# A hybrid transformer block with expert retrieval on one core: gate tables built beside 59 blocks in place of 83, weight splits three pieces ahead, and a rearranged end

## The chip, the cores and the metric

The kernel runs on one core of one Trainium2 chip. The metric is the device time of one launch in microseconds. Engines: TensorE (PE, with PEld for its weight loads), VectorE (DVE), ScalarE (ACT), GpSimd (POOL) and SyncE (SP). They run their own instruction streams and meet at semaphores; transfers between DRAM and the on-chip memory are queued by SP, ACT and POOL.

## The reference

For 512 tokens of width 2048: an input projection, a gated MLP over chunks and a windowed attention in parallel, an output projection with residual, and then the part that takes most of the time, a mixer that retrieves 128 of 16384 experts for each token:

```python
def peer(h, w_query, sub_keys, expert_down, expert_up):
    q = (xf @ w_query).reshape(T, PEER_HEADS, 2, D_QUERY // 2)
    s1 = jnp.einsum('thd,kd->thk', q[:, :, 0], sub_keys[0])
    s2 = jnp.einsum('thd,kd->thk', q[:, :, 1], sub_keys[1])
    v1, i1 = lax.top_k(s1, PEER_TOPK)
    v2, i2 = lax.top_k(s2, PEER_TOPK)
    cand = (v1[..., :, None] + v2[..., None, :]).reshape(T, PEER_HEADS, PEER_TOPK * PEER_TOPK)
    top_v, flat = lax.top_k(cand, PEER_TOPK)
    experts = e1 * N_KEYS + e2
    gates = jax.nn.softmax(top_v, axis=-1)
    ...
        u = jnp.take(expert_down, ec, axis=0)
        a = jax.nn.gelu(jnp.einsum('cd,chkd->chk', xc, u), approximate=False)
        vt = jnp.take(expert_up, ec, axis=0)
        return jnp.einsum('chk,chkd->cd', gc * a, vt)
```

After it the residual is added and a last norm gives the output. Everything is float32.

## The kernel before, in words

**Two ways through the experts.** 352 tokens (`TD`) go through all 16384 experts densely: 128 blocks `down(b)` of 128 experts each (`a = gelu(h @ down)`), and 16 chunks `up(c)` of 8 blocks each, which multiply `gate * a` with the `up` weights into the accumulator `accT`. The gate is zero where an expert was not chosen. The other 160 tokens (a full block of 128 and one of 32) fetch only the rows that they chose, in 640 *units*: one indirect transfer of 512 KB by POOL (L706) and one VectorE instruction over 128x1024 (L720 for the down rows, L732 for the up rows). The units are two jobs, 512 for the block of 128 tokens and then 128 for the 32. A unit's row lands in one of 4 buffers `row` or, once the tables are done, one of `MORE_ROWS` = 4 buffers `more`.

**The weight stream.** Every dense product is made of three float32r products (L166, L167, L168) from halves `hi` and `lo` of weight and data. `Stream` brings the weights in pieces of 512 KB: SP loads `wraw`, ScalarE casts it to `whi` (L143), and VectorE or GpSimd subtracts to get `wlo` (L145; a *split* below). A block takes 2 pieces and 48 matmuls of 352 columns, a chunk 16 pieces and 4 *quarters* of 96 matmuls. `W.get()` hands out a piece and has the next 2 split; each kind of buffer holds 4.

**Gate tables.** 88 *quads* of 4 tokens: 4 VectorE instructions `p2` (L860), 4 Abs and one Relu on ScalarE (L865, L867), 8 products on TensorE (L873) and 2 copies on ScalarE into `stage` (L886), which go to `g_dram`. They are run beside the first `OPEN` blocks. In a chunk, `make_ga` multiplies `a` by the gate (VectorE, L994), casts to `gah` (ScalarE, L998) and subtracts to `gal` (VectorE, L999).

**Order.** TensorE's order is written out: `NPRE` blocks first, their `a` spilled to `a_dram` and read back later, then chunks, with the remaining blocks between chunks, 8 for each, once a chunk needs them. After block `OPEN - 1` the table buffers are released, and the accumulator, the gates' buffers and `more` are allocated in their place (`open_late`).

**Pacing.** `Pace` decides what stands in the other engines' streams between TensorE's groups. `vector` is a balance of VectorE time: each group of matmuls adds 0.98 of its own time, each piece of work takes its estimate off. `use_pool` gives a split to GpSimd when the balance is at or below zero, and GpSimd's own balance allows. A unit is emitted when `gap` ns of TensorE work have gone by since the last. A table step is emitted when its share of the time left to `OPEN` has gone by.

```python
    def use_pool(self):
        if self.vector > 0.0 or self.pool < 0.0:
            self.vector -= 1250.0
            return False
```

**The end.** In the last chunk, `rows_out(q)` turns a finished quarter of `accT` back to rows on TensorE (tile `dn`, 2 buffers, L1145), VectorE adds the residual (`xr`, L1148), ScalarE squares for the norm (L1135) and `gf` is multiplied in (L1137). `last_norm` scales and sends a token block out (L1122 to L1131). `rest_of_first` does that for the 128 fetched tokens in quarter 1 (`yf`, L1160), `rest_of_last` for the 32 in quarter 3: their sums lie in four parts, which are brought by 8 transfers and added by 8 VectorE instructions (L1184).

Of the kernel before, what the change touches and what calls it, by code (L numbers as in the profile page):

```python
# [19 lines left out]
P = 128  # L20
D = 2048
# [15 lines left out]
NCHUNK = NK // CB  # L37
NPRE = 88
OPEN = NPRE - 5
TG = 32  # L40
NTG = TD // TG
BIG = 3.0e38
COL_NS = 0.4505
MORE_ROWS = 4


class Pace:


    def __init__(self):  # L50
        self.hot, self.paced, self.units = deque(), deque(), deque()
        self.later = []
        self.vector = self.pool = self.wait = self.due = self.left = 0.0
        self.gap = 2600.0
        self.held = False
# [4 lines left out]
    def use_pool(self):  # L60
        if self.vector > 0.0 or self.pool < 0.0:
            self.vector -= 1250.0
            return False
        self.vector -= 500.0
        self.pool -= 2500.0
        return True
# [8 lines left out]
    def step(self, ns):  # L75
        self.vector = max(min(self.vector + 0.98 * ns, 3000.0), -4000.0)
        self.pool = min(self.pool + ns, 3000.0)
# [80 lines left out]
def block_kernel(ctx, tc, a, out):  # L158
# [675 lines left out]
    def table(b, choice):  # L834
# [15 lines left out]
        def quad(n):  # L850
            def f():
# [17 lines left out]
                def products():  # L869
# [5 lines left out]
                    if n % 8 == 0:  # L875
                        if "pool" not in stage:
                            psc.release()
                            stage["pool"] = tc.alloc_tile_pool(name="pst", bufs=1, side="right",
                                                               reuse_waits="tile")
                        for h in range(2):  # L880
                            stage[h] = stage["pool"].tile([P, NK // 2, TG], F32, name="stage",
                                                          bufs=4)
                    o = 4 * (n % 8)
# [4 lines left out]
                    if n % 8 == 7:  # L888
                        for h in range(2):
# [98 lines left out]
    def make_ga(b):  # L988
        if b not in a_sb:
            return  # L990
        t = a_sb.pop(b)
        t3 = t.rearrange("p (g t) -> p g t", g=NTG)
        g = g4[b // 4][:, :, (b % 4) * TG:(b % 4 + 1) * TG]
        nc.vector.tensor_tensor(t3, t3, g, op=OP.mult)  # L994
        pace.spend(1060.0)
# [19 lines left out]
    def down(b):  # L1015
        ps = ps2.tile([P, TD], F32, name="dn", bufs=2)
        for h in range(2):
            hi, lo = W.get()
            for k in range(8):
# [22 lines left out]
    def up(c):  # L1042
# [3 lines left out]
        for q in range(4):  # L1046
# [14 lines left out]
            for i in range(2):  # L1061
                w = W.get()
                for j in (2 * i, 2 * i + 1):
# [7 lines left out]
                tick()  # L1071
            if last and q == 1:
                rest_of_first()
            if last and q == 2:
                pace.drain()
                rest_of_last = finish_last()
            if last and q == 3:
                rest_of_last()
            if last and q:
# [4 lines left out]
            w = [W.get(1), W.get(2)]  # L1084
            for m in range(4):
                for j in range(4, 8):
                    multiply(m, j, w[j // 2 - 2])
                y = accT[:, 4 * q + m, :]
                if c == 0:
                    nc.scalar.copy(y, ps[m])  # L1090
                else:
                    nc.vector.tensor_add(y, ps[m], y)  # L1092
                    pace.spend(520.0)
            if nxt is not None and q == 3:
                for j in range(6, 8):
# [43 lines left out]
    def rows_out(q):  # L1139
        cols = slice(q * 512, (q + 1) * 512)  # L1140
        for b in range(ND):
# [7 lines left out]
            square(b, n, y, q, nc.vector if q == 3 else nc.gpsimd)  # L1149
            if q == 3:  # L1150
                last_norm(b, n, y, o_rows[b + 1][:n])

# [12 lines left out]

    def finish_last():
        n = EX
        x = late["fin"].tile([P, D], F32, name="xf")
        nc.scalar.dma_start(x[:n], x_dram[NB - 1][P - n:])
        parts = []  # L1170
        for h in range(2):
            cols = slice(h * D // 2, (h + 1) * D // 2)
            for s in range(P // EX):
                if h:
                    t = pg.tile([P, D // 2], F32, name="row", bufs=4)
                else:
                    t = late["p"].tile([P, D // 2], F32, name="more", bufs=MORE_ROWS)
                eng = nc.sync if s % 2 else nc.scalar
                eng.dma_start(t[:n], y_dram[1][s * n:(s + 1) * n, cols])
                parts.append((t, cols))  # L1180

        def rest():
            for t, cols in parts:
                nc.vector.tensor_add(x[:n, cols], x[:n, cols], t[:n])  # L1184
            for q in range(4):
                square(NB, n, x, q, nc.vector)
            last_norm(NB, n, x, o_rows[NB - 1][P - n:])
        return rest

    def spread():  # L1190
        left = sum(2 * 24 for k, i in order if k == "d" and i >= OPEN)
        left += sum(384 for k, i in order if k == "u")
        pace.gap = (left * TD * COL_NS - 45e3) / len(pace.units)

    for kind, i in order:
        if kind == "u":
            up(i)
            continue
        down(i)
        if i == OPEN - 1:  # L1200
# [3 lines left out]
            open_late()  # L1204
            spread()
            opening.extend([
# [82 lines left out]
```

## Time and profile before

| what | value |
| --- | --- |
| median of 3 runs | 3058.1 us (3056.44 to 3060.74) |
| the profiled execution | 3053.1 us, of which the trace spans 3051.4 us |
| TensorE busy / VectorE / GpSimd / ScalarE | 2867.4 / 2260.2 / 1474.2 / 1152.7 us |
| bytes moved | 779.91 MB, mean 256 GB/s |
| mean granted TensorE clock | 0.976 |

Busy time is that of the engine's own instructions. In the rows below, a window's columns are its width, each engine's busy time with the number of instructions, the granted clock as a share of full speed, the share of the 16 DMA engines' time that was busy, and GB/s.

### The profile page before, as it was taken

The page shows a single profiled execution, that of the slowest core. Times are in us where ns is not written, and L with a number is a line of the kernel's source. Part 1 is how long each engine was busy: PE and PEld are TensorE (multiplying, and loading weights), DVE is VectorE, ACT ScalarE, POOL GpSimd, SP SyncE. Part 2 cuts the span into 40 slices and gives each one's busy share as a digit, 9 for nine tenths or more (in the row PEclk, how much of TensorE's full clock was granted, in tenths as well). Part 3 has the DMA queues.
Part 4 walks back from the last instruction along what each step waited for, and adds up shares of the span by engine and source line. Part 5 has one row for each costly group of instructions (what it writes and reads, how often), then busy time and mean ns, then how long its engine had stood idle before and what let it go on. Part 6 is the DMA issues. An engine that isn't in the chain of part 4 may idle for free. (4 is left out here: it accounts for less than half of the span.)

```text
span 3051.4 us, 44502 instructions
## 1 busy us (share of the span) xinstructions
PE 2867.4 (94%) x16925; PEld 2727.1 (89%) x16925; DVE 2260.2 (74%) x3359; ACT 1152.7 (38%) x1932; POOL 1474.2 (48%) x998
## 2 busy tenths in 40 slices
PE   7999999999999899999989999999999999999976
PEld 6888878799999899999988999998999999999975
DVE  3125642469947999999957888887788889778865
ACT  3244432222333456767824222322232323323223
POOL 2132100123578667777645666666665444344432
PEclk9999999999999999999999999999999999999987
DMA  5221242422379678978798999999989999899983
GB/s 191 86 83 56 76 162 90 146 90 87 122 260 343 215 264 293 317 261 316 264 333 323 357 347 342 337 334 329 353 330 347 334 334 360 315 332 335 347 306 104
DMA packets 265190, 779.91 MB, mean 256 GB/s; under 512 B 25488, under 2 KB 94416, under 8 KB 259408
## 3 DMA queue, kind: packets, MB, share of 16 engines
q1 hardware_dynamic: 151952, 382.75, 36.7%
q0 software_dynamic: 92160, 335.59, 29.0%
q10 hardware_dynamic: 20864, 58.74, 5.0%
q8 instruction: 133, 2.18, 0.3%
q14 instruction: 81, 0.66, 0.1%
HBM read 726.20 MB, written 50.77 MB: 255 GB/s over the span
## 5 line engine op out<-in xcount | busy, mean ns | idle before, releaser
L145 POOL TENSOR_TENSOR wlo<-wraw,whi 128x1024 fp32r<-128x1024 f32 x284 | 701.0, 2477 | 849.1 <-ACT whi L143 813.3
L143 ACT CAST whi<-wraw 128x1024 fp32r<-128x1024 f32 x628 | 641.2, 1048 | 679.3 <-PE up L167 326.8
L168 PE MATMUL up<-gah,wlo 128*128 128x352 f32 x2048 | 673.9, 329 | 47.2 <-POOL wlo L145 44.0
L166 PE MATMUL up<-gah,whi 128*128 128x352 f32 x2048 | 675.2, 330 | 19.9 <-DVE accT L1092 19.2
L145 DVE TENSOR_TENSOR wlo<-wraw,whi 128x1024 fp32r<-128x1024 f32 x344 | 462.1, 1350 | 305.5 <-ACT whi L143 303.8
L166 PE MATMUL dn<-h2d,whi 128*128 128x352 f32 x2048 | 667.3, 326 | 15.2 <-ACT whi L143 15.2
L168 PE MATMUL dn<-h2d,wlo 128*128 128x352 f32 x2048 | 669.7, 327 | 5.8 <-POOL wlo L145 3.6
L167 PE MATMUL up<-gal,whi 128*128 128x352 f32 x2048 | 668.9, 327 | 0.0
L167 PE MATMUL dn<-h2d,whi 128*128 128x352 f32 x2048 | 667.0, 326 | 0.0
L168 PEld LDWEIGHTS up<-gah,wlo 128*128 128x128 f32 x2048 | 394.0, 192 | 56.9 <-POOL wlo L145 53.2
L166 PEld LDWEIGHTS up<-gah,whi 128*128 128x128 f32 x2048 | 394.4, 193 | 27.5 <-DVE accT L1092 18.0
L166 PEld LDWEIGHTS dn<-h2d,whi 128*128 128x128 f32 x2048 | 390.8, 191 | 16.1 <-ACT whi L143 16.1
L168 PEld LDWEIGHTS dn<-h2d,wlo 128*128 128x128 f32 x2048 | 389.5, 190 | 10.3 <-POOL wlo L145 6.9
L167 PEld LDWEIGHTS up<-gal,whi 128*128 128x128 f32 x2048 | 394.7, 193 | 0.0
L167 PEld LDWEIGHTS dn<-h2d,whi 128*128 128x128 f32 x2048 | 389.7, 190 | 0.0
L720 DVE SCALAR_TENSOR_TENSOR row<-row,half_row 128x1024 f32<-128x1024 f32 x236 | 282.6, 1211 | 70.0 <-DMA row<-in_down_rows,idx 55.7
L860 DVE SCALAR_TENSOR_TENSOR p<-iota,eT,gT 128x256 fp32r<-128x256 f32 x352 | 317.0, 959 | 1.9 <-PE tr L873 1.9
L706 POOL DMA_INDIRECT row<-in_down_rows,idx x236 | 249.3, 1056 | 140.5 <-DVE row L720 88.7
L706 POOL DMA_INDIRECT more<-in_up_rows,idx x160 | 184.4, 1152 | 162.0 <-DVE half_row L732 136.3
L706 POOL DMA_INDIRECT row<-in_up_rows,idx x160 | 182.9, 1143 | 145.3 <-DVE half_row L732 115.7
L732 DVE SCALAR_TENSOR_TENSOR half_row<-more,wgt,half_row 128x1024 f32<-128x1024 f32 x160 | 205.1, 1282 | 1.5 <-DMA more<-in_up_rows,idx 0.3
L732 DVE SCALAR_TENSOR_TENSOR half_row<-row,wgt,half_row 128x1024 f32<-128x1024 f32 x156 | 200.0, 1282 | 1.7 <-DMA row<-in_up_rows,idx 0.3
(201 smaller groups left out, 3755.7 us busy)
## 6 DMA issues: line engine op xcount, KB each, us to landing
wraw<-in_down SPq DMA_DIRECT2D x256, 512.0 KB, 5.6
wraw<-in_up SPq DMA_DIRECT2D x256, 512.0 KB, 7.0
wraw<-in_win SPq DMA_DIRECT2D x52, 512.0 KB, 3.8
g_dram<-stage ACTq DMA_DIRECT2D x22, 1024.0 KB, 8.2
g<-g_dram SPq DMA_DIRECT2D x32, 704.0 KB, 9.3
wraw<-in_wout SPq DMA_DIRECT2D x32, 512.0 KB, 3.7
wraw<-in_wq SPq DMA_DIRECT2D x32, 512.0 KB, 3.7
aa<-a_dram SPq DMA_DIRECT2D x88, 176.0 KB, 9.1
```

The costliest lines, as they stand in the source:

```text
L143: self.nc.scalar.copy(hi, src)
L145: eng.tensor_sub(lo, src, hi.bitcast(F32))
L166: nc.tensor.matmul(ps, wh, xh, start=start, stop=False)
L167: nc.tensor.matmul(ps, wh, xl, start=False, stop=False)
L168: nc.tensor.matmul(ps, wl, xh, start=False, stop=stop)
L706: nc.gpsimd.indirect_dma_start(out=t, out_offset=None, in_=src, in_offset=bass.IndirectOffsetOnAxis(ap=idx[i][:, j, h:h + 1], axis=0))
L720: nc.vector.scalar_tensor_tensor(t, t, 1.0, half_row, op0=OP.mult, op1=OP.mult, accum_out=dots[i][:, j, h:h + 1])
L732: nc.vector.scalar_tensor_tensor(half_row, t, wgt[i][:, j:j + 1], half_row, op0=OP.mult, op1=OP.add)
L860: nc.vector.scalar_tensor_tensor(p2[:, j], iota[:, None, :].to_broadcast([P, 2, P]), t[:, 1, k:k + 1], hl[:, k, :, None].to_broadcast([P, ...
```

## The change

`NPRE` goes from 88 to 64, and `OPEN`, which is `NPRE - 5`, from 83 to 59. So the same 88 quads stand beside 59 blocks, 24 fewer `a` tiles are spilled and read back, chunks start 24 blocks earlier, and chunks 7 to 14 have 8 blocks between them in place of chunks 10 to 14. `W.get(3)` asks for three splits ahead instead of two in `down` and in the first half of a quarter. In `Pace` the refill goes from 0.98 to 1.12 and the threshold of `use_pool` from 0 to -300, which leaves more splits on VectorE; during the last two groups of a quarter nothing is emitted (`held`). The gap of units is 2300 in place of 2600 while the tables are made, and is worked out anew at each chunk from what is left. `MORE_ROWS` is 3. In the last chunk `rest_of_first` moves from quarter 1 to quarter 2; the four parts of the 32 tokens are brought by 2 transfers and summed by 4 products with a matrix of ones, one ahead of each group of quarter 3; and the three last norms stand behind all three last adds. `NTG` and `FULL` change nothing at 352 = 11 x 32 tokens.

```diff
-NPRE = 88
+NPRE = 64
 OPEN = NPRE - 5
...
-MORE_ROWS = 4
+MORE_ROWS = 3
...
-        self.gap = 2600.0
+        self.gap = 2300.0
...
-        if self.vector > 0.0 or self.pool < 0.0:
+        if self.vector > -300.0 or self.pool < 0.0:
...
-        self.vector = max(min(self.vector + 0.98 * ns, 3000.0), -4000.0)
+        self.vector = max(min(self.vector + 1.12 * ns, 3000.0), -4000.0)
...
-            hi, lo = W.get()
+            hi, lo = W.get(3)
...
-                w = W.get()
+                w = W.get(3)
...
-            if last and q == 1:
+            if last and q == 2:
                 rest_of_first()
-            if last and q == 2:
                 pace.drain()
-                rest_of_last = finish_last()
-            if last and q == 3:
-                rest_of_last()
+                steps_of_last.extend(finish_last())
...
             for m in range(4):
+                pace.held = m > 1
+                if last and q == 3 and steps_of_last:
+                    steps_of_last.pop(0)()
...
-            if q == 3:
-                last_norm(b, n, y, o_rows[b + 1][:n])
+        if q == 3:
+            for b in range(ND):
+                n = min(P, TD - b * P)
+                last_norm(b, n, late["x"][b], o_rows[b + 1][:n])
...
+        def piece(q):
+            cols = slice(q * 512, (q + 1) * 512)
+            ps = ps2.tile([P, 512], F32, name="dn", bufs=2)
+            nc.tensor.matmul(ps[:n], ones, parts[q // 2][:, q % 2 * 512:(q % 2 + 1) * 512],
+                             start=True, stop=True)
+            nc.vector.tensor_add(x[:n, cols], ps[:n], x[:n, cols])
+            square(NB, n, x, q, nc.gpsimd)
+            if q == 3:
+                last_norm(NB, n, x, o_rows[NB - 1][P - n:])
...
+    def spread(at):
+        left = sum(48 if k == "d" else 384 for k, i in order[at:]) * TD * COL_NS
+        if pace.units:
+            pace.gap = max(2000.0, (left - 110e3) / len(pace.units))
```

What stands in GpSimd's stream at the start of chunk 5, before (`DMA` rows are units' transfers, `wlo` is a split):

```order
L706 DMA row<-in_up_rows,idx_4077 128x1024 x2
L145 TENSOR_TENSOR wlo<-wraw,whi 128x1024
L706 DMA row<-in_up_rows,idx_4077 128x1024
L706 DMA more<-in_up_rows,idx_4077 128x1024 x2
L145 TENSOR_TENSOR wlo<-wraw,whi 128x1024
L706 DMA more<-in_up_rows,idx_4077 128x1024 x2
L706 DMA row<-in_up_rows,idx_4077 128x1024 x4
L145 TENSOR_TENSOR wlo<-wraw,whi 128x1024
```

The same chunk on GpSimd after the change (the units are earlier ones, of the down rows):

```order
L707 DMA row<-in_down_rows,idx_4077 128x1024
L146 TENSOR_TENSOR wlo<-wraw,whi 128x1024
L707 DMA row<-in_down_rows,idx_4077 128x1024 x3
L707 DMA more<-in_down_rows,idx_4077 128x1024 x3
L707 DMA row<-in_down_rows,idx_4077 128x1024 x4
L146 TENSOR_TENSOR wlo<-wraw,whi 128x1024
L707 DMA more<-in_down_rows,idx_4077 128x1024
L146 TENSOR_TENSOR wlo<-wraw,whi 128x1024
```

In the whole chunk 8 splits stood on GpSimd and 8 on VectorE; now 3 and 13, with 23 units both times. Over the kernel GpSimd's splits go from 284 to 166 and VectorE's from 344 to 462.

VectorE's stream beside the last table blocks, before: quads alternate with units, and only the last ten quads follow one another.

```order
L720 SCALAR_TENSOR_TENSOR row,dots_4083<-row,half_row 128x1024
L860 SCALAR_TENSOR_TENSOR p_13318<-iota,eT,gT 128x256 x4
L720 SCALAR_TENSOR_TENSOR row,dots_4083<-row,half_row 128x1024
L860 SCALAR_TENSOR_TENSOR p_13377<-iota,eT,gT 128x256 x4
L720 SCALAR_TENSOR_TENSOR row,dots_4083<-row,half_row 128x1024
L860 SCALAR_TENSOR_TENSOR p_13432<-iota,eT,gT 128x256 x4
L860 SCALAR_TENSOR_TENSOR p_13466<-iota,eT,gT 128x256 x4
```

The same place after the change, with what stands ahead of it:

```order
L721 SCALAR_TENSOR_TENSOR row,dots_4083<-row,half_row 128x1024
L861 SCALAR_TENSOR_TENSOR p_10829<-iota,eT,gT 128x256 x4
L861 SCALAR_TENSOR_TENSOR p_10873<-iota,eT,gT 128x256 x4
L848 TENSOR_TENSOR gT<-tr,gT 128x128
L146 TENSOR_TENSOR wlo<-wraw,whi 128x1024
L861 SCALAR_TENSOR_TENSOR p_10931<-iota,eT,gT 128x256 x4
L861 SCALAR_TENSOR_TENSOR p_10954<-iota,eT,gT 128x256 x4
```

From there 34 quads follow one another with no unit and no VectorE split between them: 4 to a block in the last 8 table blocks (51 to 58), whose 16 splits all stand on GpSimd. Of the 640 units 153 stood ahead of the end of the tables, and 85 do now; the last stood in the last chunk, and now stands in block 121.

The last rows of VectorE's stream, before (`xr` by token block, 128, 128 and 96 rows):

```order
L1092 TENSOR_TENSOR accT<-up,accT 128x352 x4
L1148 TENSOR_TENSOR xr_26854<-dn,xr_26854 128x512
L1137 TENSOR_TENSOR xr_26854<-xr_26854,gf 128x512
L1122 TENSOR_REDUCE sf<-ss_26853 128x1
L1128 TENSOR_SCALAR xr_26854<-xr_26854,rstd 128x1024
L1148 TENSOR_TENSOR xr_26856<-dn,xr_26856 128x512
L1137 TENSOR_TENSOR xr_26856<-xr_26856,gf 128x512
```

And after the change:

```order
L1156 TENSOR_TENSOR xr_26812<-dn,xr_26812 128x512
L1145 TENSOR_TENSOR xr_26812<-xr_26812,gf 128x512
L1156 TENSOR_TENSOR xr_26814<-dn,xr_26814 128x512
L1145 TENSOR_TENSOR xr_26814<-xr_26814,gf 128x512
L1156 TENSOR_TENSOR xr_26816<-dn,xr_26816 96x512
L1145 TENSOR_TENSOR xr_26816<-xr_26816,gf 96x512
L1130 TENSOR_REDUCE sf<-ss_26811 128x1
L1136 TENSOR_SCALAR xr_26812<-xr_26812,rstd 128x1024
L1130 TENSOR_REDUCE sf<-ss_26811 128x1
L1136 TENSOR_SCALAR xr_26814<-xr_26814,rstd 128x1024
```

The adds of all three blocks stand first, each still followed at once by its own `gf` product; the reduces and scales follow one block after the other.

## Rows read from the trace of the kernel before

**Rows 1.** Windows of the stages: tables, opening with chunk 0, chunks 1–9, rest, last.

```profile
784.00:1540.50 756.50, 733.61 (x4699) 728.32 (x4699) 674.65 (x991) 430.22 (x885) 558.55 (x318) 0.98 0.78 271
1540.50:1666.50 126.00, 108.62 (x626) 105.64 (x624) 83.09 (x124) 40.27 (x60) 51.88 (x43) 0.92 0.95 350
1666.50:2287.60 621.10, 577.42 (x3456) 565.47 (x3457) 511.75 (x638) 181.79 (x221) 396.19 (x275) 0.97 0.91 339
2287.60:2929.10 641.50, 622.43 (x3842) 618.20 (x3841) 542.71 (x619) 200.00 (x245) 288.41 (x242) 0.99 0.93 337
2929.10:3051.40 122.30, 73.81 (x434) 71.65 (x432) 69.61 (x83) 35.95 (x62) 27.24 (x28) 0.80 0.48 175
```

**Rows 2.** Windows: ten blocks, a block with four quads' products, a quarter.

```profile
791.72:868.52 76.80, 76.80 (x482) 76.80 (x481) 52.06 (x83) 26.24 (x32) 50.63 (x20) 1.00 0.48 161
1510.31:1521.58 11.27, 11.27 (x82) 11.27 (x82) 10.84 (x17) 10.19 (x27) 5.20 (x2) 1.00 0.81 299
1961.08:1976.36 15.28, 15.28 (x99) 15.28 (x97) 14.27 (x13) 3.24 (x4) 11.02 (x10) 1.00 1.02 397
```

**Rows 3.** TensorE's waits, whole span: us in total, times, longest us.

```profile
PE up L168 <- POOL wlo L145: 44.0, 25, 3.8
PE dn L1145 <- DVE xr L1148: 25.6, 4, 16.1
```

**Rows 4.** Timeline of VectorE and GpSimd, a table block: start, us, instruction, idle ahead.

```profile
1031.85 6.43 DVE L860 SCALAR_TENSOR_TENSOR p<-iota,eT,gT 128x256 fp32r<-128x256 f32 x4
1039.35 1.66 DVE L860 SCALAR_TENSOR_TENSOR p<-iota,eT,gT 128x256 fp32r<-128x256 f32 x4
1031.73 2.38 POOL L145 TENSOR_TENSOR wlo<-wraw,whi 128x1024 fp32r<-128x1024 f32 x1
```

**Rows 5.** Groups, chunk 5 and then 2488.5 to 2612: busy us, mean ns, idle ahead.

```profile
L145 DVE TENSOR_TENSOR wlo<-wraw,whi 128x1024 fp32r<-128x1024 f32 x8 | 16.7, 2088 | 1.0 <-ACT whi L143 1.0
L999 DVE TENSOR_TENSOR gal<-aa,gah 128x352 fp32r<-128x352 f32 x8 | 4.2, 526 | 4.7 <-ACT gah L998 4.7
...
L145 DVE TENSOR_TENSOR wlo<-wraw,whi 128x1024 fp32r<-128x1024 f32 x30 | 36.5, 1220 | 4.8 <-ACT whi L143 4.4 <-PE dn L168 0.4
```

**Rows 6.** Waits of SP's queue in chunk 5 (L132 loads a piece).

```profile
SPq L132 <- POOL wlo L145: 28.8, 8, 6.7
```

**Rows 7.** Windows: chunk 5, chunk 10, eight blocks with chunk 12.

```profile
1942.70:2011.60 68.90, 63.75 (x385) 62.60 (x385) 59.37 (x64) 19.82 (x24) 45.17 (x32) 0.98 0.92 339
2295.70:2363.80 68.10, 63.49 (x385) 62.62 (x385) 56.95 (x56) 18.06 (x19) 38.99 (x32) 0.97 0.98 362
2612.00:2751.00 139.00, 127.80 (x770) 126.40 (x770) 113.46 (x169) 43.94 (x53) 58.04 (x50) 0.96 0.92 326
```

**Rows 8.** The page's DMA queues: pieces and loads (q1), units (q0).

```profile
q1 hardware_dynamic: 151952, 382.75, 36.7%
q0 software_dynamic: 92160, 335.59, 29.0%
```

**Rows 9.** Windows: quarters 1 and 3 of the last chunk.

```profile
2949.40:2984.43 35.03, 18.96 (x109) 18.67 (x109) 18.35 (x20) 9.60 (x20) 9.44 (x9) 0.76 0.54 212
3001.57:3029.27 27.70, 18.84 (x112) 18.53 (x111) 19.04 (x24) 7.30 (x17) 4.50 (x5) 0.82 0.05 10
```

**Rows 10.** Timeline of VectorE in the last chunk and the end.

```profile
2963.82 2.29 DVE L1160 TENSOR_TENSOR yf<-yf,xf 128x2048 f32<-128x2048 f32 x1 [7.72 <-DMA xf<-x_dram]
2972.84 0.75 DVE L1128 TENSOR_SCALAR yf<-yf,rstd 128x1024 f32<-128x1024 f32 x1 [3.51 <-POOL rstd L1126]
3004.48 4.95 DVE L1184 TENSOR_TENSOR xf<-xf,more 32x1024 f32<-32x1024 f32 x4
...
3030.22 0.69 DVE L1148 TENSOR_TENSOR xr<-dn,xr 128x512 f32<-128x512 f32 x1 [0.42 <-PE dn L1145]
3031.76 0.69 DVE L1137 TENSOR_TENSOR xr<-xr,gf 128x512 f32<-128x512 f32 x1 [0.85 <-ACT junk L1135]
3033.47 0.75 DVE L1128 TENSOR_SCALAR xr<-xr,rstd 128x1024 f32<-128x1024 f32 x1 [0.95 <-POOL rstd L1126]
```

More of the change, by code (lines that the diff above doesn't have):

```diff
@@ L37 @@
 NCHUNK = NK // CB
-NPRE = 88
+NPRE = 64
 OPEN = NPRE - 5
 TG = 32
-NTG = TD // TG
+NTG = -(-TD // TG)
+FULL = TD // TG
 BIG = 3.0e38
 COL_NS = 0.4505
-MORE_ROWS = 4
+MORE_ROWS = 3
 class Pace:
@@ L882, in products @@
                                                           bufs=4)
+                            used = TD - b * P - 4 * n
+                            if used < TG:
+                                nc.gpsimd.memset(stage[h][:, :, used:], 0.0)
                     o = 4 * (n % 8)
@@ L887, in products @@
                                        ps[:, :, k].rearrange("p t k -> p k t"))
-                    if n % 8 == 7:
+                    if n % 8 == 7 or 4 * (n + 1) == TD - b * P:
                         for h in range(2):
@@ L991, in make_ga @@
         t = a_sb.pop(b)
-        t3 = t.rearrange("p (g t) -> p g t", g=NTG)
         g = g4[b // 4][:, :, (b % 4) * TG:(b % 4 + 1) * TG]
-        nc.vector.tensor_tensor(t3, t3, g, op=OP.mult)
+        if FULL < NTG:
+            end = t[:, FULL * TG:]
+            nc.gpsimd.tensor_tensor(end, end, g[:, FULL, :TD - FULL * TG], op=OP.mult)
+        t3 = t[:, :FULL * TG].rearrange("p (g t) -> p g t", g=FULL)
+        nc.vector.tensor_tensor(t3, t3, g[:, :FULL], op=OP.mult)
         pace.spend(1060.0)
@@ L1093, in up @@
                     pace.spend(520.0)
+            pace.held = False
             if nxt is not None and q == 3:
@@ L1171, in finish_last @@
         for h in range(2):
[L1172 to L1195, printed above, removed]
+            t = pg.tile([P, D // 2], F32, name="row", bufs=4)
+            nc.sync.dma_start(t, y_dram[1][:, h * D // 2:(h + 1) * D // 2])
+            parts.append(t)
+        ones = late["fin"].tile([P, EX], F32, name="ones")
+        nc.vector.tensor_reduce(ones, ident.rearrange("p (s m) -> p m s", m=EX), axis=AX.X, op=OP.add)
+        def piece(q):
[7 more added lines that the diff above has]
+                last_norm(NB, n, x, o_rows[NB - 1][P - n:])
+        return [lambda q=q: piece(q) for q in range(4)]
+    steps_of_last = []
+    def spread(at):
+        left = sum(48 if k == "d" else 384 for k, i in order[at:]) * TD * COL_NS
+        if pace.units:
+            pace.gap = max(2000.0, (left - 110e3) / len(pace.units))
+    for at, (kind, i) in enumerate(order):
         if kind == "u":
+            spread(at)
             up(i)
@@ L1204, in block_kernel @@
             open_late()
-            spread()
+            spread(at)
             opening.extend([
```

## The prediction

> **What bounds the kernel now.** I read the windows of the stages first [rows 1]: TensorE is busy for 86 to 97% of each up to 2929 us, VectorE for 89% of the table stage, and the DMA engines for 0.91 to 0.95 after it. So TensorE's work is the floor, and what can be won is the time it loses. Its work has a measured pace where nothing disturbs it: a block takes 7.68 us (ten in 76.80), a quad's products add 0.90 to a block ((11.27 - 7.68) / 4), a quarter takes 15.28, so a chunk 61.1 [rows 2]. The change leaves this work as it is, but for 4 small products. I therefore keep a ledger of lost time: a stage's width less this pace.
>
> - Tables, blocks 0 to 82 with 88 quads: 756.5 - 637.4 - 79.2 = 39.9.
> - Opening, 5 blocks and chunk 0: 126.0 - 38.4 - 61.1 = 26.5.
> - Chunks 1 to 9, nothing between them: 621.1 - 549.9 = 71.2, or 7.9 each.
> - 40 blocks and chunks 10 to 14: 641.5 - 307.2 - 305.5 = 28.8, of which 139.0 - 122.6 = 16.4 in the period of chunk 12, where the second job of units begins [rows 7].
> - Chunk 15: its window runs to 3029.3, so 100.1 - 61.1 = 39. The tail after TensorE: 22.1.
>
> That is 227.5 of the span of 3051.4 [rows 1, 2]. The waits then say on whom [rows 3]: the `up` products wait 44.0 us for splits on GpSimd, and the turned rows of the end (`dn`) 25.6 us in 4 waits for VectorE.
>
> **Why a split on GpSimd hurts.** Beside GpSimd's splits, a VectorE split takes 2088 ns on the mean; in a stretch of 123.5 us where all are on VectorE, 1220 [rows 5]. Four `p2` take 6.43 us while a split of 2.38 us starts on GpSimd, and 1.66 without one [rows 4]. So the two engines hinder each other, and eight splits of a chunk moved to GpSimd save VectorE little. The late halves also keep the raw buffers: SP's loads wait 28.8 us for GpSimd in chunk 5 [rows 6], while the DMA engines idle for 8% of it [rows 7].
>
> **The change, stage by stage.** *Tables.* 59 blocks and 88 quads at pace are 453.1 + 79.2 = 532.3. The decoding and the quads that cost 39.9 remain, so I keep 39.9; 68 fewer units and the looser pacing could only take from it (low bound 35). New are 8 blocks in a row with 4 quads each and both splits on GpSimd. The trace has one window of a block with 4 quads: VectorE is busy for 10.84 of its 11.27 us, ScalarE for 10.19 with 27 instructions [rows 2]. A full block has 4 x 7 of quads, 2 casts and a GELU, so 31: 10.19 x 31 / 27 = 11.7, and the transfers that ScalarE issues come on top. I take 12.5 against 11.27, about 1.3 a block, 10 in all: lost 50. The other bound is VectorE at the mean of its two rates, (6.43 + 1.66) / 2 = 4.05 a quad in the 34 that follow one another, against 2.82 at pace: 42 more, so 92 [rows 4]. I take 50, since the one window that has the new mix lies near it.
>
> *Opening.* The same allocations, first gates and first chunk, at a DMA share of 0.95 already [rows 1]: 26, unchanged.
>
> *Chunks 1 to 6.* 13 splits on VectorE, 3 on GpSimd, 23 units as before. VectorE's busy time was 59.37 [rows 7]; its 8 splits took 16.7. Thirteen at 1.22 with three hindered ones at 2.09 take 18.5, so it becomes about 61, and `gal` still waits 4.7 for ScalarE [rows 5]. VectorE alone then needs near 65.9 a chunk, against 61.1 at pace and 68.9 now. Splits three ahead cover what comes late within a quarter, not a balance that is full. I take 5 lost a chunk, 30 in all, for 6 chunks in place of 9 (bounds 2.2, where only a quarter's worst waits remain, and 7.9 as now).
>
> *The rest: 64 blocks and 8 chunks, 7 to 14.* Splits were on VectorE here already. A chunk with its 8 blocks gets 49 to 50 units in place of 47 or 48. The second job still begins in chunk 12, so its 16.4 stay; the other four periods lost 12.4, 3.1 each, and seven such would lose 22: 38 (bounds 21, where the job begins unnoticed, and 65, where all lose about as much as a chunk by itself, 7.9). One row buffer less means a row asked for 6 units ahead in place of 7, at a gap near 2.4 some 14 us, against 1.38 of transfer a unit [rows 8]: nothing, unless its transfer is late by that.
>
> *Chunk 15.* Quarter 1 lost 35.0 - 15.3 = 19.8 [rows 9]: `yf` stood in VectorE's stream ahead of the residual adds and waited 7.72 for its transfer, then for GpSimd's `rstd`; behind it stood the `xr` adds, and TensorE waited 16.1 for these [rows 3, 10]. In quarter 2 the transfer has landed, but the chain from `yf` to its scale, 2963.82 to 2973.6, still stands ahead of the adds: 10 lost there at most. Quarter 3 lost 27.7 - 15.3 = 12.4, eight adds of 32x1024 taking 9.9 [rows 9, 10]. Four products and four adds of half the width replace them. The trace has no plain float32 product 512 wide: I bound it by a quad's product, 0.90 / 8 = 0.11 us, and by eight products of a block, 8 x 7.68 / 48 = 1.28. Nearer the upper one, being the wider, at 0.9, the four cost 3.6; with the adds I take 6. Their two transfers stand on SP behind the last pieces, and the last unit that they read stands 7 blocks ahead, so these cost nothing; if they came late, quarter 3 would wait as quarter 1 did, 10 to 20. With 4 for quarters 0 and 1 the chunk loses 20 in place of 39.
>
> *Tail.* Per token block the chain is 0.69 for the add, 0.85 of wait for the square, 0.69 for `gf`, 1.02 for the reduce and `rstd`, 0.75 for the scale: 4.0 us, 12 for three [rows 10]. Side by side, each `gf` product still stands behind its own add and waits for its square, 3 x 2.23, and each reduce behind the scale ahead of it, 3 x 1.77: 12.0. Nothing is won, and the outputs leave bunched: 23 for 22.1.
>
> Sum of lost time: 50 + 26 + 30 + 38 + 20 + 23 = 187 in place of 227.5, so 40.5 less. From the profiled execution's 3053.1 this gives 3012.6. That execution was 5.0 under the median of 3058.1, so for the median I say **3017**.
>
> **Do the transfers fit?** From the tables' end to chunk 15 they took 0.95 x 126 + 0.91 x 621.1 + 0.93 x 641.5 = 1281 us of all engines [rows 1]. A unit takes 29.0% x 3051.4 / 640 = 1.38, a piece 36.7% x 3051.4 x 0.524 / 382.75 = 1.53 [rows 8]. The stage gains 79 units (109) and 48 pieces (74) and drops 24 reads of `a` (13): 1451. TensorE's pace there is 69 x 7.68 + 15 x 61.1 = 1446, my sum 1540: share 0.94. The highest share over a whole chunk is 0.98, at 362 GB/s [rows 7], and I take that share as the ceiling. So the stage is close to a second bound. The stage's 350 x 126 + 339 x 621.1 + 337 x 641.5 = 471 MB become 533 with these units and pieces, 346 GB/s in my sum. The Trainium skill ("DMA: Bandwidth & Descriptors", Specifications) puts the limit of HBM for one core at about 358 GB/s; by it the stage could not come under 1489 us, an estimate, and the time not under 2966. That limit is not what this trace shows, 362 GB/s over 68.1 us, 1% above it.
>
> **Rivals.**
> *Later part nearly at TensorE's pace.* If splits in time let the engines reach 0.98, the stage takes 1451 / 0.98 = 1481, 59 less: 2958. For it: SP's waits for splits in chunk 5, and chunk 10's share of 0.98. Against it: VectorE's balance near 66 a chunk, and that even chunk 10 lost 7.0.
> *Slower: transfers bind.* The chunks start 24 blocks earlier and the units that had room in the table stage (share 0.78) move where there was 0.93. If the share stays at 0.90, since a row buffer less and four raw buffers don't bridge a late piece, the stage takes 1612: 3089. It ends where it was at 1451 / (1540 + 40.5) = 0.918, about what chunks 1 to 9 had. For it: 0.91 over 621 us. Against it: that 0.91 came with late splits.
> *Tables bound by VectorE.* The upper bound above, 92 lost: 3059, no gain.
> *The change doesn't do it.* Chunks 1 to 6 keep 7.9, and quarters 2 and 3 of chunk 15 give back what quarter 1 gains: 17 + 14 more, 3048.
>
> **How the numbers follow.** My forecast 0.45, from 2990 to 3045 with the bounds above; nearly at pace 0.24; transfers bind 0.14; tables bound 0.09; doesn't do it 0.08. The first two are faster. A difference under 0.2%, 3052 to 3064, is about what a measurement of this kernel can't tell from none. The tables' case lies in there, with half of its spread above; of the last, centred at 3048, half is in there. So same is 0.10, slower 0.16, faster 0.74. The range 2947 to 3074 leaves out the best of the second case and the worse half of the third.
>
> **What would show it.** The window from the first block to the last with tables: 582 us if I am right, 625 if VectorE binds there. Chunks 1 to 6: 66 each; TensorE's waits for GpSimd's splits there under 15 us in place of 44.0. The DMA share between tables and chunk 15: 0.94. Quarter 1 of chunk 15 near 17, quarter 2 near 25, quarter 3 near 21. The prediction is wrong if the share there stays under 0.92 with TensorE waiting for `whi`, or if the eight dense table blocks take 13 us or more each.

## The result and the profile after

The changed kernel takes 3031.8 us, the median of 4 runs (3028.1 to 3036.6), against 3059.4 for the kernel before on the same chip: a ratio of 0.9907, with a 95% interval of 0.9888 to 0.9926. The forecast was 3017, with a range of 2947 to 3074. The profiled execution took 3028.1 us, and its trace spans 3026.4.

The stages of the changed kernel, windows as in [rows 1]: tables (blocks 0 to 58), opening with chunk 0, chunks 1 to 6, the 64 blocks with chunks 7 to 14 (two windows, the second the last 7 blocks), and chunk 15 with the tail.

```profile
783.70:1362.50 578.80, 548.14 (x3548) 542.75 (x3547) 515.73 (x897) 369.95 (x810) 333.49 (x185) 0.97 0.70 244
1362.50:1480.70 118.20, 106.85 (x626) 103.31 (x625) 76.04 (x115) 40.34 (x63) 50.53 (x43) 0.96 0.96 354
1480.70:1905.00 424.30, 388.24 (x2304) 383.06 (x2305) 337.50 (x543) 121.63 (x149) 202.37 (x159) 0.96 0.90 334
1905.00:2867.00 962.00, 938.92 (x5810) 934.22 (x5809) 853.18 (x932) 300.73 (x365) 438.99 (x377) 0.99 0.96 352
2867.00:2920.80 53.80, 53.80 (x339) 53.80 (x338) 28.66 (x32) 20.64 (x28) 0.00 (x0) 1.00 0.43 149
2920.80:3026.40 105.60, 75.16 (x441) 69.12 (x439) 43.53 (x62) 34.22 (x60) 27.01 (x27) 0.86 0.45 161
```

With the pace of [rows 2] this gives the same ledger of lost time as in the prediction, in us. Each entry is a window's width less its blocks at 7.68, quads at 0.90 and chunks at 61.1; the chunks stand by themselves from 1 to 6 (or 1 to 9). The last three rows are experiments that are told below.

| kernel | tables | opening | chunks alone | rest | chunk 15 | tail | sum |
| --- | --- | --- | --- | --- | --- | --- | --- |
| before | 39.9 | 26.5 | 71.2 (9) | 28.8 | 39.0 | 22.2 | 227.6 |
| forecast | 50 | 26 | 30 (6) | 38 | 20 | 23 | 187 |
| after | 46.5 | 18.7 | 57.7 (6) | 35.4 | 20.3 | 24.2 | 202.8 |
| before with `NPRE` = 64 alone | 46.8 | 17.7 | 34.2 (6) | 41.4 | 44.7 | 22.1 | 206.9 |
| before with the new end alone | 45.3 | 25.0 | 74.7 (9) | 31.2 | 25.8 | 24.1 | 226.1 |
| after with `MORE_ROWS` = 4 | 45.5 | 18.5 | 13.1 (6) | 35.9 | 20.8 | 24.2 | 158.0 |

Sums answer to spans: after is 24.8 under before, and its span 25.0. One execution strays from another: the table stage of the code of before lost 39.9, 45.3 and 42.9 us in three traces, that of the changed kernel 45.5 to 47.3 in three and 61.0 in a fourth. So a stage counts here where two or more kernels agree on it.

The waits of TensorE over the span answer to [rows 3]:

```profile
PE up L167 <- DVE accT L1099: 56.9, 29, 11.9
PE dn L169 <- POOL wlo L146: 13.5, 5, 4.7
PE dn L1153 <- DVE xr L1156: 8.9, 3, 8.2
```

And in the kernel before, for the first of these:

```profile
PE up L166 <- DVE accT L1092: 19.2, 18, 4.9
```

The `up` products no longer wait for GpSimd's splits (44.0 before); they wait for the adds to `accT`, which cost 19.2 before and cost 56.9 now. That wait has grown in the place of the one removed, and 36.1 of it lies in chunks 1 to 6. The waits of GpSimd and VectorE there say what is late:

```profile
POOL wlo L146 <- ACT whi L144: 131.7, 13, 11.9
DVE row L721 <- DMA row<-in_down_rows,idx: 21.7, 7, 3.9
DVE more L721 <- DMA more<-in_down_rows,idx: 14.6, 5, 3.3
PE up L167 <- DVE accT L1099: 36.1, 16, 4.0
```

VectorE waits 36.3 us for rows of units, 12 times, two in each chunk, and TensorE waits 36.1 for VectorE. One such case in chunk 5, from the timelines of GpSimd, ScalarE and VectorE:

```profile
1790.96 0.94 POOL L707 DMA_INDIRECT row<-in_down_rows,idx  x1 [0.60 <-DVE row L721]
1793.03 1.21 DVE L721 SCALAR_TENSOR_TENSOR row<-row,half_row 128x1024 f32<-128x1024 f32 x1
1799.59 0.49 ACT L1005 CAST gah<-aa 128x352 fp32r<-128x352 f32 x1 [7.73 <-DVE aa L1001]
1801.49 2.95 ACT L144 CAST whi<-wraw 128x1024 fp32r<-128x1024 f32 x3
1803.62 2.45 POOL L146 TENSOR_TENSOR wlo<-wraw,whi 128x1024 fp32r<-128x1024 f32 x1 [11.73 <-ACT whi L144]
1806.23 1.82 POOL L707 DMA_INDIRECT row<-in_down_rows,idx  x1 [0.16 <-DVE more L721]
1811.69 0.52 DVE L1099 TENSOR_TENSOR accT<-up,accT 128x352 f32<-128x352 f32 x1
1815.30 1.22 DVE L721 SCALAR_TENSOR_TENSOR row<-row,half_row 128x1024 f32<-128x1024 f32 x1 [3.08 <-DMA row<-in_down_rows,idx]
1816.44 1.38 DVE L1099 TENSOR_TENSOR accT<-up,accT 128x352 f32<-128x352 f32 x3
```

From 1791.9 to 1803.6 nothing runs on GpSimd: the next instruction is a split whose `whi` ScalarE has not cast. That cast stands in ScalarE's stream behind `gah` casts for the next chunk, which wait 7.73 us for VectorE's `aa`. All twelve holds of more than 8 us in these six chunks (8.8 to 11.9) have such `gah` casts just ahead of the late `whi`; no run puts the `whi` casts ahead of them. The transfers of units stand behind the split, and the first goes out at 1806.2. Its buffer had come free at 1794.2, when VectorE ended the seventh unit before, and its row was wanted at 1812.2: of these 18.0 us the hold, with the split itself, took 12.0, and the transfer needed 9.1 from its issue until VectorE could start. So VectorE waits 3.08 us for the row, and three adds to `accT` that stand behind it come late together. The four PSUM tiles of these adds are what the next quarter's first products need.

### The profile page after: what moved, and what is told of

Its sections match the earlier page's. It is cut to its first block, busy times and chain, and to the rows that moved or that the text cites. A ratio compares the mean times of both kernels' runs of the same rounds, so it can differ in the third digit from the quotient of the medians.

```text
span 3026.4 us, 44414 instructions
## 1 busy us (share of the span) xinstructions
PE 2861.0 (95%) x16933; PEld 2722.1 (90%) x16933; DVE 2231.6 (74%) x3470; ACT 1152.0 (38%) x1932; POOL 1203.9 (40%) x884
## 3 DMA queue, kind: packets, MB, share of 16 engines
q1 hardware_dynamic: 148592, 378.95, 36.1%
## 4 chain that ended last, share of the span: by engine, by line
PE 60%; DVE 15%; issue 9%; ACT 7%; DMA 6%; POOL 2%; ACTq 0%; SPq 0%; DVEq 0%; POOLq 0%
PE up L167 8%; PE up L168 8%; PE up L169 8%; PE acc L167 7%; PE acc L169 7%; PE acc L168 7%; DVE half_row L733 6%; PE dn L167 4%; PE dn L169 4%; PE dn L168 4%; DMA row<-in_down_rows,idx 3%; ACT whi L144 3%; DVE wlo L146 2%; PE tr L874 2%; DMA more<-in_down_rows,idx 1%
## 5 line engine op out<-in xcount | busy, mean ns | idle before, releaser
L146 DVE TENSOR_TENSOR wlo<-wraw,whi 128x1024 fp32r<-128x1024 f32 x462 | 564.4, 1234 | 308.7 <-ACT whi L144 308.0
L146 POOL TENSOR_TENSOR wlo<-wraw,whi 128x1024 fp32r<-128x1024 f32 x166 | 414.6, 2503 | 863.1 <-ACT whi L144 839.5
L167 PE MATMUL up<-gah,whi 128*128 128x352 f32 x2048 | 676.7, 330 | 66.1 <-DVE accT L1099 56.9
L707 POOL DMA_INDIRECT row<-in_down_rows,idx x221 | 238.1, 1077 | 213.1 <-DVE row L721 159.4
L707 POOL DMA_INDIRECT row<-in_up_rows,idx x182 | 205.0, 1126 | 262.6 <-DVE half_row L733 252.9
L721 DVE SCALAR_TENSOR_TENSOR row<-row,half_row 128x1024 f32<-128x1024 f32 x221 | 264.3, 1214 | 52.5 <-DMA row<-in_down_rows,idx 43.9
L861 DVE SCALAR_TENSOR_TENSOR p<-iota,eT,gT 128x256 fp32r<-128x256 f32 x352 | 225.5, 704 | 15.5 <-PE tr L874 15.5
L733 DVE SCALAR_TENSOR_TENSOR half_row<-row,wgt,half_row 128x1024 f32<-128x1024 f32 x181 | 232.5, 1284 | 2.0
L707 POOL DMA_INDIRECT more<-in_up_rows,idx x138 | 167.4, 1213 | 160.4 <-DVE half_row L733 141.8
L1005 ACT CAST gah<-aa 128x352 fp32r<-128x352 f32 x128 | 62.3, 487 | 372.6 <-DVE aa L1001 334.8
```

The lines of the kernel that those rows point to most:

```text
L146: eng.tensor_sub(lo, src, hi.bitcast(F32))
L167: nc.tensor.matmul(ps, wh, xh, start=start, stop=False)
L707: nc.gpsimd.indirect_dma_start(out=t, out_offset=None, in_=src, in_offset=bass.IndirectOffsetOnAxis(ap=idx[i][:, j, h:h + 1], axis=0))
L721: nc.vector.scalar_tensor_tensor(t, t, 1.0, half_row, op0=OP.mult, op1=OP.mult, accum_out=dots[i][:, j, h:h + 1])
L733: nc.vector.scalar_tensor_tensor(half_row, t, wgt[i][:, j:j + 1], half_row, op0=OP.mult, op1=OP.add)
L861: nc.vector.scalar_tensor_tensor(p2[:, j], iota[:, None, :].to_broadcast([P, 2, P]), t[:, 1, k:k + 1], hl[:, k, :, None].to_broadcast([P, ...
```

## The experiments

Each ratio is to the kernel before on the same chip, with its 95% interval.

**No split on GpSimd from chunk 0 on.**

```diff
+        if p >= 116 + 2 * NPRE:
+            pace.vector -= 1250.0
+            return False
         return pace.use_pool()
```

> The changed kernel, but from chunk 0 on every split stands on VectorE (in chunks 1 to 6 that moves 3 of 16 a chunk; the table stage is as it was). Theory A: chunks 1 to 6 lose 9.6 us each because a split on GpSimd waits up to 11.7 us for its whi, holds the units' transfers queued behind it, VectorE then waits 3 to 4 us for a row and accT behind it keeps TensorE waiting. Without these splits a chunk takes 64 to 66 us in place of 70.7, and the kernel 2995 to 3005. Rival B: VectorE's time is simply full there (56.3 busy, 4.7 of waits for gah, and 3 x 1.22 more with the splits); then a chunk stays at 70 to 72 and the kernel at 3030 to 3040.

Measured: 3020.1 us, 0.9867 (0.9840 to 0.9893). Chunks 1 to 6 took 63.1 to 65.5 us each in place of 66.8 to 72.3, and VectorE had no wait for rows there. Their window in this kernel:

```profile
1493.57:1880.92 387.35, 372.27 (x2304) 367.89 (x2305) 342.36 (x538) 120.44 (x148) 145.96 (x127) 1.00 0.95 348
```

Against the changed kernel's window above, VectorE is busy for 4.9 us more, and the six chunks are 37.0 us shorter, so VectorE was not full. The kernel won less than that and missed its range, since the rest lost 59.3 in place of 35.4; a second kernel with this edit (below) showed the same 24 us. The traces show one difference that may be its cause, which no run tests. A split on VectorE takes 1250 off the pacing's balance and one on GpSimd 500, so fewer units came in chunks 1 to 6 (127 transfers in place of 139), and 386 in place of 375 were left for the rest. There VectorE is busy for 901 us in place of 882, and TensorE waits 41.0 in place of 23.1 for VectorE and ScalarE. In the changed kernel and the six made from it with the tables beside 59 blocks the loss of the rest rises with its units: 28.4 and 31.7 us with 366 and 367 of them, 35 to 36 with 374 and 375, 59 to 60 with 385 and 386, 67.5 with 409. The table stage's 61.0 in this profiled execution, the slowest of its six, was not seen again with the same code.

**One row buffer more.**

```diff
-MORE_ROWS = 3
+MORE_ROWS = 4
```

> The changed kernel with MORE_ROWS = 4 as before, so that rows are asked for 7 units ahead in place of 6. Theory A: the hold on GpSimd's queue is bridged by one more gap of 2.45 us, VectorE's waits of 3 to 4 us for a row in chunks 1 to 6 shrink to about 1, and the kernel takes 3012 to 3022. Rival B, VectorE full: no change, 3028 to 3036.

Measured: 2991.3 us, 0.9780 (0.9751 to 0.9808), some 40 us under the changed kernel, twice what the theory had given it, so its range was missed too. Its window and waits in chunks 1 to 6:

```profile
1480.41:1860.16 379.75, 372.52 (x2304) 366.95 (x2305) 334.90 (x540) 121.50 (x149) 209.73 (x158) 1.00 0.99 372
```

```profile
POOL wlo L146 <- ACT whi L144: 104.8, 12, 9.4
PE up L167 <- DVE accT L1099: 7.0, 13, 0.8
DVE row L721 <- DMA row<-in_down_rows,idx: 0.9, 2, 0.6
DVE more L721 <- DMA more<-in_down_rows,idx: 0.7, 1, 0.7
```

GpSimd's splits still wait 104.8 us for `whi` in place of 131.7, 9.4 at the longest in place of 11.9, but VectorE no longer runs out of rows (1.6 us in place of 36.3), and the stage is 44.6 us shorter. All other stages agree with the changed kernel within 1.

**The pacing of before.** Threshold 0 and refill 0.98, all else as changed:

```diff
-        if self.vector > -300.0 or self.pool < 0.0:
+        if self.vector > 0.0 or self.pool < 0.0:
...
-        self.vector = max(min(self.vector + 1.12 * ns, 3000.0), -4000.0)
+        self.vector = max(min(self.vector + 0.98 * ns, 3000.0), -4000.0)
```

> The changed kernel with the pacing of before (threshold 0, refill 0.98), splits still asked for three ahead; GpSimd gets 295 splits in place of 166. Theory A: more splits on GpSimd that wait for whi hold the units' transfers oftener, chunks 1 to 6 lose 10 or more each, and the kernel takes 3035 to 3060. Rival B: VectorE has room again, chunks lose 5 to 7, and the kernel takes 3005 to 3022.

Measured: 3068.9 us, 1.0023 (1.0004 to 1.0042). The time came out dearer still than the theory had it, and for other reasons: chunks lost 7.9 each, less than with the new pacing and not the 10 or more of the theory, while the tables lost 62.6 and the rest 67.5. Beside three splits ahead the looser pacing goes with some 16 us less in the tables and 32 less in the rest, by one trace of each. Beside two ahead the tables go the other way: 46.8 with the old pacing and 61 to 63 with the new, both below.

**The new end on the kernel before.**

```diff
-            if last and q == 1:
+            if last and q == 2:
                 rest_of_first()
-            if last and q == 2:
                 pace.drain()
-                rest_of_last = finish_last()
-            if last and q == 3:
-                rest_of_last()
+                steps_of_last.extend(finish_last())
```

(with the four products and the last norms behind all adds, as in the change)

> The kernel before with the new end alone: rest_of_first in quarter 2, the 32 tokens' parts by 2 transfers and 4 products with ones, last norms behind all adds. Theory A: the end alone gives what the ledger of the two traces says, 39 - 20 = 19 in chunk 15 less 2 in the tail, so 3040 to 3045 against 3059. Rival: the gain there comes from the units that no longer reach into chunk 15; then the end alone gives at most 8, 3051 or more.

Measured: 3049.7 us, 0.9963 (0.9942 to 0.9984), between the two. Chunk 15 lost 25.8 in place of 39.0, and the tail 24.1 in place of 22.2. Quarter 0 of that chunk still lost 5.0, as before, since units still reach into it; in the changed kernel it loses 0.1. So 13 us of chunk 15's 19 are the new end's, and 5 are the units'.

**Two splits ahead again**, with three rows and with four.

```diff
-            hi, lo = W.get(3)
+            hi, lo = W.get()
...
-                w = W.get(3)
+                w = W.get()
```

> The changed kernel with splits asked for two ahead again, everywhere (MORE_ROWS stays 3). Theory A: what costs in chunks 1 to 6 is the few rows ahead together with a GpSimd split that holds the queue; the trace of before shows such holds (10.2 us) with two ahead as well, so chunks still lose 8 or more each and TensorE waits for halves on top: 3030 to 3050. Rival C: asking three ahead put the split in front of the transfers and made the hold; then chunks lose 3 to 5 each and the kernel takes 2995 to 3015.

> The changed kernel with MORE_ROWS = 4 and splits asked for two ahead. Theory A: with rows in time, what two ahead costs is TensorE's waits for halves from GpSimd, which were 61 us in the run with three rows and two ahead; the table stage loses 16 more and the chunks 4 to 6 each, 3010 to 3030. Rival: three ahead gives nothing once the rows are in time, 2988 to 2998.

Measured: 3041.6 us with three rows, 0.9929 (0.9900 to 0.9957), and 3040.1 with four, 0.9918 (0.9895 to 0.9940). Chunks 1 to 6 lose 10.5 and 9.9 each, and the tables 62.7 and 61.4. TensorE's waits in chunks 1 to 6 with four rows, and VectorE's for rows with three:

```profile
PE up L169 <- POOL wlo L146: 38.4, 22, 4.9
PE up L167 <- ACT whi L144: 2.0, 1, 2.0
```

```profile
DVE more L721 <- DMA more<-in_down_rows,idx: 3.8, 3, 1.7
DVE row L721 <- DMA row<-in_down_rows,idx: 0.9, 2, 0.7
```

Here the halves from GpSimd are late for TensorE itself. With three rows VectorE's waits for rows came to 4.7 us in place of 36.3, so the total lies in the range given, but the theory's reason for it, that holds run VectorE out of rows with two ahead as well, fell. With four rows the range was missed, as the chunks lost about twice the 4 to 6 given. A fourth row is worth nothing here, 40 us with three ahead.

**The kernel before with the new end and three rows.**

```diff
-MORE_ROWS = 4
+MORE_ROWS = 3
```

> The kernel before with the new end (measured as 0.9963 of before) and MORE_ROWS = 3 in place of 4. Theory A: there too a GpSimd split waits for its whi (10.2 us at the longest) and holds the units' transfers, so with a row less the 9 chunks lose 4 to 7 more each: 3080 to 3115. Rival C: the hold is made by asking three ahead; then it stays at 3045 to 3055.

Measured: 3055.1 us, 0.9983 (0.9962 to 1.0004), within the interval of the same kernel with four rows (0.9963). Rival C had it right, at the upper edge of its range: with two ahead and a gap of 2612 ns, three rows cost little or nothing.

**Both cures together**: four rows and no split on GpSimd from chunk 0 on.

> The changed kernel with MORE_ROWS = 4 and no split on GpSimd from chunk 0 on, the two edits that each took the loss of chunks 1 to 6 away. Theory A: they cure the same thing, a row that comes late behind a held queue, so together they give what four rows give alone: chunks near 63, 2982 to 2996. Rival: they are separate costs and add up: below 2980.

Measured: 3022.6 us, 0.9872 (0.9841 to 0.9904). Chunks 1 to 6 lost 21.0 in all, as with the second cure alone, so the two cure one thing. The total missed, since the rest lost 59.6 again, as it did without GpSimd's splits and with three rows.

**Tables beside 83 blocks again**, with three rows, and with four and a gap of 2600.

```diff
-NPRE = 64
+NPRE = 88
```

> The changed kernel with NPRE = 88 again, so with the tables beside 83 blocks and chunks 1 to 9 with nothing between them; all else as changed. Theory A: 9 chunks that lose 9.6 in place of 6 cost 29 more, and three periods with blocks fewer give back 12, the table stage loses 25 to 40 as before: 3030 to 3050. Rival D: the earlier tables are where the gain outside the end comes from, since they move units from the stage with room; then 3050 to 3070. A third outcome, under 3025, would say that the 59 blocks cost time.

> The changed kernel with MORE_ROWS = 4, NPRE = 88 again (tables beside 83 blocks) and a gap of 2600 in the table stage. Theory A with its addition, that the tables' place only moves units between stages and gives nothing by itself: table stage loses 35 to 45, chunks 1 to 9 lose 2 to 3.5 each, the rest 12 to 25, so 2970 to 2995, level with or under four rows beside 59 blocks (2991). Rival D, that the tables beside 59 blocks are a gain of their own: 3005 or more.

Measured: 3035.5 us, 0.9908 (0.9880 to 0.9937), and 3016.3 us, 0.9838 (0.9814 to 0.9863). The first total lies in its range and its parts don't: the tables lost 109.3 and the 9 chunks only 3.4 each. The second missed its range and came where rival D had put it, as the tables lost 87.0. Their window there, and what TensorE waited for:

```profile
785.08:1588.74 803.66, 749.32 (x4700) 738.25 (x4699) 712.81 (x1157) 437.59 (x886) 523.39 (x330) 0.96 0.82 292
```

```profile
PE tr L874 <- DVE p L861: 28.6, 16, 7.5
PE dn L169 <- POOL wlo L146: 11.6, 8, 4.7
```

The looser pacing puts 206 units and 46 splits on VectorE beside the tables, where there were 152 and 4; the `p2` come late, and TensorE with them. In the kernel with three rows the chunks lose little although three splits stand on GpSimd in each there too, and wait as long for `whi`:

```profile
POOL wlo L146 <- ACT whi L144: 182.0, 18, 11.9
```

Its gap is 2.7 to 2.8 us, as more units are done ahead, and VectorE waits 4.6 us for rows in all nine chunks.

**Tables beside 67 blocks, with four rows** (`NPRE = 72`).

> The changed kernel with MORE_ROWS = 4 and NPRE = 72, so the tables beside 67 blocks. Theory A: fewer blocks with four quads (4 to 8 us less in the table stage) and some 20 units fewer behind it; one chunk more stands by itself at 2.2: 2975 to 2992, level with or a little under 59 blocks. Rival: the place of the tables is critical and 8 blocks more cost 10 or more: over 3000.

Measured: 3006.2 us, 0.9796 (0.9771 to 0.9820), on a chip where the kernel before took 3066.8. That is the ratio of 59 blocks with four rows within the intervals, and missed the range in us, where the rival's (over 3000) held. Chunks 1 to 7 lost 2.1 each; the tables lost 69.4, the opposite of what was expected of them.

**`NPRE` = 64 alone, on the kernel before.**

```diff
-NPRE = 88
+NPRE = 64
```

> The kernel before with NPRE = 64 alone (tables beside 59 blocks, chunks 24 blocks earlier; the old pacing, two splits ahead, four rows, the old end). Theory A: 24 blocks fewer for the same quads make the table stage lose 60 or more, the units moved behind it lose as much again in the 8 periods of a chunk and 8 blocks, and 3 chunks fewer give back 24: 3065 to 3100, slower than before. Rival D: the earlier tables are a gain alone: 3035 to 3050.

Measured: 3037.6 us, 0.9906 (0.9883 to 0.9930). The theory's addition, that the tables' place gives nothing by itself, fell outright: this one number gives as much as the whole change, and rival D had it right. The windows of its tables, opening, chunks 1 to 6, and rest:

```profile
784.67:1363.78 579.11, 556.44 (x3549) 550.69 (x3547) 477.99 (x799) 365.88 (x811) 347.77 (x171) 0.96 0.61 214
1363.78:1480.97 117.19, 107.85 (x625) 105.40 (x625) 76.96 (x112) 40.57 (x61) 64.60 (x49) 0.94 0.96 364
1480.97:1881.79 400.82, 379.62 (x2305) 371.71 (x2305) 326.65 (x520) 121.70 (x148) 292.32 (x194) 0.98 0.96 356
1881.79:2903.90 1022.11, 992.05 (x6149) 985.03 (x6148) 892.57 (x995) 319.41 (x392) 478.26 (x402) 0.99 0.95 348
```

Against [rows 1] the tables lose 7 more, the opening 9 less, chunks alone 37 less, the rest 13 more and chunk 15 loses 6 more. Of the 37, 25 belong to the three chunks that no longer stand alone, and 13 of these come back in the rest: a chunk by itself lost some 8 us, one with 8 blocks a little more than 5. The other 12 are chunks 1 to 6 themselves, which lose 5.7 each in place of 7.7. Why they and the opening lose less is not shown.

## Why the prediction was right, and where it was wrong

The direction and the range held, and four of the six terms of the ledger came within 4 us. The sum was 15.8 us too good. One term was 27.7 too good, and the others gave 11.9 of it back, which is luck in the main: 7.3 of that are the opening's, for which the prediction had worked out no change.

**Chunks 1 to 6: 30 forecast, 57.7 measured.** The step that failed stands in the part on the rest: that one row buffer less costs nothing, "some 14 us, against 1.38 of transfer a unit". Its "unless its transfer is late by that" is what came, but in chunks 1 to 6, and the sum had no term for it. The step compared the lead of a row with a unit's share of the DMA engines' time, and left out how long the transfer can stand in GpSimd's queue; from issue to landing a unit took 7.0 to 8.5 us at the median in the kernel before already, not 1.38. In the case shown above the lead was 18.0 us, and the hold and the transfer took 21.1. One buffer more would have given the row the buffer freed at 1790.7, 21.5 us ahead, an estimate from the same timeline. Four edits each took the loss of rows away: a row more, no split in that queue, two splits ahead in place of three, or fewer units (a gap of 2.75 us in place of 2.48, so 16.5 of the pacing's time for six units in place of 14.9). So it takes all of these at once: splits on GpSimd, asked for early, three rows, and the denser units. Each cure but the row has its own price, in halves that come late, in the rest, or in the tables.

**VectorE's balance, "near 65.9 a chunk"**, was wrong too, and hid the first error, since it gave the 5 us of loss a cause. With four rows a chunk takes 63.1 to 63.6, with VectorE busy for 334.90 of 379.75 us in the six. The busy time that I added up, 61 a chunk, came out at 55.8 to 56.3.

**Splits.** That they would be in time for TensorE was right: 0 us of waits for GpSimd's splits in the `up` products, for the 44.0 before. It is the three ahead that does it, not their being on VectorE: with two ahead and the new pacing the 40 us are back.

**Tables: 50 forecast, 46.5.** The dense blocks were read rightly as a matter of ScalarE. The window of blocks 52 to 58:

```profile
1268.43:1362.54 94.11, 86.51 (x594) 84.09 (x593) 74.15 (x123) 86.72 (x231) 34.85 (x15) 0.96 0.53 190
```

ScalarE is busy for 86.72 of its 94.11 us, and TensorE waits there for nothing but ScalarE's `p`, 7.6 us. At pace that window is 53.8 + 28.8, so 11.5 were lost, for 10 forecast; ahead of it 35.0 were lost, the low bound of the 39.9. The loss did not come block by block, as 12.5 for each: blocks 52 to 55 ran at pace, 11.27, and 9.7 were lost in block 58 alone, where the quads that are behind are finished. That VectorE would bind here, the upper bound, was not seen: its `p2` took 704 ns each over the stage, 959 before.

**Opening: 26 forecast, 18.7.** Not costed, and not settled by these runs beyond this: `NPRE` alone gives 17.7, and all kernels with the tables beside 59 blocks lie between 16.5 and 20.2.

**The rest: 38 forecast, 35.4.** Chunk 12, where the second job begins, took 76.3 us, and between 72 and 81 in all kernels made from the changed one with the tables beside 59 or 67 blocks.

**Chunk 15: 20 forecast, 20.3.** The quarters answer to [rows 9]:

```profile
2920.77:2936.15 15.38, 15.38 (x97) 15.38 (x97) 6.04 (x8) 4.81 (x6) 0.00 (x0) 1.00 0.94 341
2936.15:2953.28 17.13, 16.78 (x110) 16.52 (x109) 8.70 (x11) 6.27 (x11) 4.79 (x3) 1.00 0.75 303
2953.28:2980.01 26.73, 18.55 (x110) 18.27 (x109) 12.00 (x15) 10.22 (x20) 10.48 (x9) 0.87 0.42 128
2980.01:3002.16 22.15, 21.80 (x120) 17.32 (x119) 9.20 (x14) 6.16 (x16) 8.04 (x7) 1.00 0.00 1
```

Forecast were about 17, 25 and 21 for quarters 1 to 3. Quarter 2 loses 11.5 to the chain of `yf`, which moved there whole, without its wait for the transfer. In quarter 3 the four products run as eight instructions of 604 ns, 4.2 us busy, for the 3.6 of the estimate.

**Tail: 23 forecast, 24.2, for a reason I did not give.** The outputs don't lose time by leaving together: from the last scale's end to the end of the span it is 9.1 us in both kernels. VectorE's timeline from the norm of the 32 tokens on, and the last scale before:

```profile
3001.61 0.15 DVE L1130 TENSOR_REDUCE sf<-ss 32x1 f32<-32x4 f32 x1 [0.85 <-ACT junk L1143]
3003.85 0.74 DVE L1136 TENSOR_SCALAR xf<-xf,rstd 32x1024 f32<-32x1024 f32 x1 [2.10 <-POOL rstd L1134]
3004.52 0.50 DVE L1099 TENSOR_TENSOR accT<-up,accT 128x352 f32<-128x352 f32 x1
3005.59 0.69 DVE L1156 TENSOR_TENSOR xr<-dn,xr 128x512 f32<-128x512 f32 x1 [0.57 <-PE dn L1153]
...
3016.57 0.75 DVE L1136 TENSOR_SCALAR xr<-xr,rstd 96x1024 f32<-96x1024 f32 x1 [0.94 <-POOL rstd L1134]
```

```profile
3041.54 0.75 DVE L1128 TENSOR_SCALAR xr<-xr,rstd 96x1024 f32<-96x1024 f32 x1 [0.94 <-POOL rstd L1126]
```

The last add to `accT` could start at 3002.2, when TensorE ends; it stands behind the 32 tokens' norm, which waits for `rstd`, and starts at 3004.5. From the first `xr` add to the last scale's end it is 11.7 us, against 12.1 before (from 3030.22 in [rows 10]), so "nothing is won" by the norms side by side was right but for 0.3.

**The rivals.** Transfers did not bind. The share between the tables and chunk 15 was 0.92, where the sum had 0.94. It was 0.94 up to block 121, behind which no unit is left and the last 7 blocks have 0.43:

```profile
1362.50:2867.00 1504.50, 1434.00 (x8738) 1420.59 (x8738) 1266.72 (x1588) 462.70 (x576) 691.89 (x577) 0.98 0.94 347
```

With four rows chunks 1 to 6 ran at 0.99 and 372 GB/s for 380 us. My ceiling of 0.98 was too low. The Trainium skill ("Perfetto Trace Analysis", Roofline) says of the 358 GB/s that a core alone can pull more, bounded by its 16 DMA engines at about 435; the trace with four rows agrees with its 372, and the 2966 us that the prediction set beside that limit was no floor. "The later part nearly at TensorE's pace" was within reach: the kernel with four rows is that case in the chunks by themselves, and takes 2991.

**What each part gave.** The tables' place alone: 0.9906. The new end alone: 0.9963. If the two multiply, which no run tests, that is 0.987. The whole change is 0.9907, so by that the rest of it (pacing, three ahead, units' gap, and a row buffer less) gave back some 0.4%, about as much as the intervals leave open; with four rows (0.9780) it adds 0.9%. The place of the tables is not a fixed gain either: the changed kernel takes 0.9907 with 59 blocks and 0.9908 with 83, and with four rows 0.9780 and 0.9838. The version with four rows beside 59 blocks is the fastest of those measured.

## What to carry to other kernels

An engine that issues transfers is not spare because it is half idle: an instruction that waits in its stream holds every transfer behind it, so the lead of a buffer is to be set against the longest hold in the issuing queue and the time from issue to landing, and not against the transfer's share of the DMA engines. Asking earlier for a piece can put a waiting instruction in front of transfers that had been in time; whoever asks earlier looks at what stands behind it on that engine, and at what its own input stands behind. And a ledger of lost time by stage, kept against a measured pace, shows which of several edits in one change works against the others, where the total alone read as a fair gain.

## What the runs showed of the hardware that was not expected

- The 16 DMA engines were busy for 0.99 of 380 us at 372 GB/s, with gathers of 512 KB and weight pieces of 512 KB mixed, and TensorE lost only 2 us in 63 meanwhile.
- A plain float32 product with a 128x32 weight and 512 columns runs as two instructions of 604 ns; a float32r product of 352 columns at pace takes 160 ns (7.68 us for 48).
- Kernels that put every split of the chunks on VectorE lost 24 us more in the stage after chunks 1 to 6, in two cases of two, with 11 units more in it. Whether these are the reason stays open.
